# Weight sums and split weight parts made in the first half and kept in DRAM, in a two-layer kernel of split fp32 products

## The chip, the cores and the metric

The kernel runs on one core of a Trainium2 chip. The metric is the device time of one execution in microseconds (us), as the median of several runs; a profiled execution gives the trace.

## The reference

What is computed is one step of a two-layer model on 2176 tokens (128 of a prompt, 2048 latent ones) of width 1024, all in fp32. Each layer is a norm, an input projection, elementwise mixing and an output projection:

```python
for l in range(DEPTH):                       # DEPTH = 2
    shift, scale, gate = adaln(cond, w_ada[l], b_ada[l])
    h = rmsnorm(x, norm_g[l]) * (1.0 + scale) + shift
    if l % 2 == 0:                           # gated linear attention | spatial gating
        out, s_f, s_b = mix_even(h @ w_in_even[j], j, gla_init[j][0], gla_init[j][1])
    else:                                    # pooling | gated short convolution
        out = mix_odd(h @ w_in_odd[j], j)    # w_in_odd: 1024 x 3072
    out = out @ w_out[l]
    x = x + gate * out
```

## The kernel before

TensorE (PE) multiplies in a rounded fp32 format, so every fp32 operand is split: `hi` is the rounded copy (made by ACT, L207) and `lo` what is left of it (a subtraction on DVE, or every third time on POOL, L208). A product is three matmuls, hi·hi, hi·lo and lo·hi (`mm3`).

**Stage 1** (`block1`) is layer 0 up to its output projection, in four blocks of 512, 512, 512 and 640 tokens. In each block 24 weight chunks of 512 or 544 KB are loaded: 16 `w0c` chunks (one `gemm_ch` each, weights stationary) and 8 `w0t` chunks (four `gemm_tok`, two chunks each, tokens stationary). `load_w` loads a chunk into one of two `raw` slots, splits it, and the parts go into one of three `hi` and three `lo` slots. So each chunk is loaded and split four times. After each chunk `tick()` advances side work written as generators: the attention, the norm of the next block, and `adalns`, which uses the same `raw` slots. **Stage 2** (`out0`) is layer 0's output projection; it stores the new x (L998) and the norm factors `r` (L1003).

**Stage 3** is layer 1, in four blocks of tokens, processed from number 3 (named `last` in the code, though it comes first) down to 0. Its input projection is made of 12 pairs of 2 x 2 blocked products in the Strassen-Winograd form: seven products instead of eight, of sums of the operand (`operand`: tiles T from `xk` and `r`, put in `ring_t`) with sums of the weights (`Weights`: S1 to S4). In the first processed block the sums are made by four POOL operations a pair (L1096), S1 is stored unsplit (`d_s`, L1098), S2 to S4 are split and both parts stored (`d_hl`, L1113); the three later blocks load S2 to S4 as parts and S1 as sum. The quarter A11, A12, A22 parts and S1 are loaded and split in every block. The output projection then loads and splits 16 halves of `wo` (`halves`) in every block.

All these DMAs go through SP's queue (`load`). The order of instructions on each engine is set by a scheduler that plans with a timeline of its own; a queue then runs strictly in that order, so an instruction that waits holds what stands behind it. Pools of SBUF are placed one above the other (or from the right); a pool that lies over an earlier one waits, tile by tile, for that one's users.

Of the kernel before, what the change touches and what calls it, by code (L numbers as in the profile page):

```python
# [86 lines left out]
def kernel(ctx: ExitStack, tc: tile.TileContext, xT, cT, w_ada, b_ada, norm_g, final_g,  # L87
# [1544 lines left out]
```

## Time and profile before

| | us |
|---|---|
| median of 3 runs | 1966.04 (1962.41 to 1968.69) |
| profiled execution, its own time | 1955.09 |
| its span in the trace | 1953.3 |
| PE busy in the span | 1761.7 |
| DVE, ACT, POOL busy | 1323.4, 931.5, 853.0 |

The span is cut by the names of the weight tiles: stage 1 runs from 31.5 to 840 us (blocks 0 to 3: `wp` tiles with `ring` operands), stage 2 to about 1078, and stage 3 to the end; in it the pairs (`ring_t` with `wh`) and the output projections (`o_oh`, `o_ol` with `wh`) of each block take turns. A window of the trace lists for such a stretch each engine's busy time, the granted clock of PE as a share of full speed, the busy share of the 16 DMA engines and what they moved.

### The profile page before, as it was taken

Reading aid. Unit: us, or ns where it says so; the run is one execution under the profiler, and the core shown is the slowest. Engines: PE = TensorE matmul, PEld = TensorE weight load, DVE = VectorE, ACT = ScalarE, POOL = GpSimd, SP = SyncE. Lnnn points to the kernel's source line nnn. Section 1 sums busy time; section 2 is a strip of 40 time slices with the busy share of each in tenths; the row PEclk is TensorE's granted clock in tenths of the full one; section 3 lists DMA queues with packets and bytes.
Section 4 is the critical chain, followed back from the end, with each engine's and each line's share of the span. In section 5 each row is a group of like instructions: output and inputs, shape, how many; then the busy total and the mean of one; then the engine's idle time right before and its main releaser. Section 6 shows DMA issues by size and latency. Waiting matters only on the chain.

```text
span 1953.3 us, 39733 instructions
## 1 busy us (share of the span) xinstructions
PE 1761.7 (90%) x15115; PEld 1595.5 (82%) x15115; DVE 1323.4 (68%) x2335; ACT 931.5 (48%) x1900; POOL 853.0 (44%) x840
## 2 busy tenths in 40 slices
PE   5999899799989999989999487879998999899996
PEld 4886787688878888977789376769998999899996
DVE  5468737965696288667664778894768476847774
ACT  4455535564555266444443544453446354634442
POOL 0444523452343133445443677783336334542433
PEclk8999999999999999998999599989999999999998
DMA  8344434354423423556543655554975397538761
GB/s 317 109 133 147 140 103 152 111 161 136 142 86 107 145 75 109 179 187 206 166 150 102 195 193 189 199 176 129 328 229 186 116 324 246 177 103 282 237 224 50
DMA packets 190127, 329.38 MB, mean 169 GB/s; under 512 B 21488, under 2 KB 64368, under 8 KB 189936
## 3 DMA queue, kind: packets, MB, share of 16 engines
q1 hardware_dynamic: 189936, 326.84, 51.5%
q8 instruction: 119, 1.95, 0.4%
q14 instruction: 72, 0.59, 0.1%
HBM read 263.90 MB, written 62.86 MB: 167 GB/s over the span
## 4 chain that ended last, share of the span: by engine, by line
PE 54%; DVE 21%; DMA 10%; ACT 5%; issue 5%; POOL 3%; SPq 1%; DVEq 0%; ACTq 0%; POOLq 0%
PE ps_g L227 49%; DMA wp_raw<-in_w0c_dram 2%; DVE wh_lo L208 2%; DVE gl_Z L535 2%; DVE ring_t L208 2%; DVE gl_L L524 1%; DVE ring_xk L361 1%; ACT wp_hi L207 1%; DVE wp_lo L208 1%; DMA wh_raw<-in_w_dram 1%; DMA wa_wa<-in_w_ada_dram 1%; PE ps_s L327 1%; DVE oA_Sb L842 1%; DVE gl_A L587 1%; DMA ring_xk<-dr_x 1%
## 5 line engine op out<-in xcount | busy, mean ns | idle before, releaser
L227 PE MATMUL ps_g<-ring_t,wh_hi 128*128 128x272 f32 (+1 forms) x2688 | 530.2, 296 | 48.2 <-ACT ring_t L207 18.1
L227 PEld LDWEIGHTS ps_g<-ring_t,wh_hi 128*128 128x128 f32 x2688 | 430.8, 192 | 60.2 <-ACT ring_t L207 19.2
L227 PE MATMUL ps_g<-ring_t,wh_lo 128*128 128x272 f32 (+1 forms) x1344 | 388.8, 296 | 16.7 <-DVE wh_lo L208 16.0
L207 ACT ACTIVATE wh_hi<-wh_raw 128x512 fp32r<-128x512 f32 x292 | 179.2, 627 | 262.9 <-PE ps_g L227 196.7
L227 PEld LDWEIGHTS ps_g<-ring_t,wh_lo 128*128 128x128 f32 x1344 | 255.3, 192 | 22.8 <-DVE wh_lo L208 20.6
L208 DVE TENSOR_TENSOR wh_lo<-wh_raw,wh_hi 128x512 fp32r<-128x512 f32 x219 | 200.0, 922 | 84.2 <-ACT wh_hi L207 75.4
L227 PE MATMUL ps_g<-ring_hh,wp_hi 128*128 128x512 f32 (+2 forms) x632 | 234.0, 370 | 6.6 <-DVE tmp_ev L784 4.8
L227 PE MATMUL ps_g<-ring_hl,wp_hi 128*128 128x512 f32 (+2 forms) x632 | 230.6, 365 | 0.0
L227 PE MATMUL ps_g<-ring_hh,wp_lo 128*128 128x512 f32 (+2 forms) x632 | 229.5, 363 | 0.0
L281 POOL TENSOR_TENSOR tmp_acc<-tmp_acc,tmp_px 128x512 f32<-128x512 f32 (+6 forms) x83 | 108.7, 1310 | 153.5 <-ACT tmp_px L280 140.9
L227 PE MATMUL ps_g<-o_oh,wh_hi 128*128 128x272 f32 (+2 forms) x512 | 149.7, 299 | 25.7 <-ACT o_oh L207 16.4
L227 PE MATMUL ps_g<-wp_hi,ring_hh 128*128 128x256 f32 (+1 forms) x528 | 156.7, 298 | 8.6 <-ACT gl_v L711 4.4
L207 ACT ACTIVATE wp_hi<-wp_raw 128x1024 fp32r<-128x1024 f32 (+1 forms) x99 | 105.3, 1064 | 118.8 <-PE ps_g L227 41.6
L535 POOL TENSOR_TENSOR gl_Z<-gl_Z 128x128 f32<-128x128 f32 x170 | 90.4, 552 | 160.7 <-DVE gl_Z L535 107.3
L227 PE MATMUL ps_g<-o_ol,wh_hi 128*128 128x272 f32 (+2 forms) x512 | 151.9, 297 | 1.5 <-DVE o_ol L208 1.5
L227 PE MATMUL ps_g<-wp_lo,ring_hh 128*128 128x256 f32 (+1 forms) x528 | 151.9, 289 | 0.8 <-POOL wp_lo L208 0.8
L208 POOL TENSOR_TENSOR wp_lo<-wp_raw,wp_hi 128x1024 fp32r<-128x1024 f32 (+1 forms) x31 | 77.0, 2483 | 172.4 <-ACT wp_hi L207 170.9
L227 PE MATMUL ps_g<-wp_hi,ring_hl 128*128 128x256 f32 (+1 forms) x528 | 151.5, 289 | 0.7 <-DVE ring_hl L377 0.7
L227 PE MATMUL ps_g<-o_oh,wh_lo 128*128 128x272 f32 (+2 forms) x512 | 150.9, 296 | 0.0
L208 DVE TENSOR_TENSOR wp_lo<-wp_raw,wp_hi 128x1024 fp32r<-128x1024 f32 (+1 forms) x68 | 90.6, 1332 | 78.5 <-ACT wp_hi L207 78.4
L227 PEld LDWEIGHTS ps_g<-ring_hh,wp_hi 128*128 128x128 f32 x632 | 121.0, 191 | 27.8 <-DVE tmp_ev L784 5.0
L208 POOL TENSOR_TENSOR wh_lo<-wh_raw,wh_hi 128x512 fp32r<-128x512 f32 x73 | 104.4, 1431 | 88.3 <-ACT wh_hi L207 86.2
(275 smaller groups left out, 4176.3 us busy)
## 6 DMA issues: line engine op xcount, KB each, us to landing
wh_raw<-in_w_dram SPq DMA_DIRECT2D x156, 256.0 KB, 3.5
wp_raw<-in_w0c_dram SPq DMA_DIRECT2D x64, 512.0 KB, 4.0
wh_hi<-dr_hl SPq DMA_DIRECT2D x108, 256.0 KB, 3.4
wh_lo<-dr_hl SPq DMA_DIRECT2D x108, 256.0 KB, 3.9
wp_raw<-in_w_ada_dram SPq DMA_DIRECT2D x32, 512.0 KB, 3.8
wh_raw<-in_wo_dram SPq DMA_DIRECT2D x64, 256.0 KB, 3.3
dr_hl<-wh_hi SPq DMA_DIRECT2D x36, 256.0 KB, 2.2
dr_hl<-wh_lo SPq DMA_DIRECT2D x36, 256.0 KB, 2.0
```

Of the source, the lines that this page charges most:

```text
L207: act(out=hi, in_=src, func=AF.Copy)
L208: (eng or lo_engine()).tensor_tensor(out=lo, in0=src, in1=hi.bitcast(F32), op=ALU.subtract)
L227: mm(out=out, lhsT=a, rhs=b, start=start and i == 0, stop=stop and i == n - 1, skip_group_check=resumed)
L281: eng.tensor_tensor(out=acc, in0=acc, in1=sq, op=ALU.add)
L327: mm(out=acc[32 * g:32 * g + 32, 0:w], lhsT=sc[:, k, :], rhs=wt[:, g * w:(g + 1) * w], start=k == 0, stop=k == KT - 1, tile_position=(0, 3 ...
L361: dve.scalar_tensor_tensor(out=xt[:, a:b], in0=xt[:, a:b], scalar=gs[:, l, k, cd:cd + 1], in1=r[:, a:b], op0=ALU.mult, op1=ALU.mult)
L524: dve.tensor_tensor(out=L, in0=qk, in1=L, op=ALU.mult)
L535: (dve if i >= 2 or s < 4 else gps).tensor_tensor(out=dst, in0=dst, in1=bc(src), op=ALU.add)
L587: dve.copy_predicated(out=A[rr_, :, rr_], mask=notl[rr_].unsqueeze(1).to_broadcast([32, 4, 32]), data=D[rr_])
L842: dve.scalar_tensor_tensor(out=S[64:P, h, 0:P], in0=Sb[0][64:P, h, 0:P], scalar=S[64:P, h, P:P + 1], in1=S[64:P, h, 0:P], op0=ALU.mult, op ...
```

## The change

1. `load_w` gets a key. For w0c chunks 4 to 15 the parts made in block 0 are stored to DRAM, for the 8 w0t chunks and w0c 0 to 3 those made in block 1: 24 chunks, 48 stores of 512 or 544 KB. Later uses (12 in block 1, 24 each in blocks 2 and 3) load the two parts straight into `hi` and `lo`: 60 loads and 60 splits become 120 loads.
2. A generator `weight_sums` makes S1 to S4 of all 12 pairs, three ticks a pair, started in block 1 after its mixer: two 512 KB loads into both `raw` slots, four sums on POOL, three copies on ACT, three subtractions on DVE, and seven stores of 256 KB. It has 36 ticks: the last 8 of block 1, the 24 of block 2, the first few of block 3.
3. Stage 3's first block then does as the later ones. `raw` has 5 slots instead of 7, `hi` and `lo` 7 instead of 6.
4. The first block of stage 3 stores the 32 split parts of its `wo` halves (`d_wo`, 256 KB each), and the three later ones load parts: 48 splits less, 48 loads more.
5. Pools change places: `xs2` lies below `tmp2`; `ring2` directly above `wh` and below `tmp3`, which then lies where stage 2's `xs2` and `tmp2` were; `yp` and `yo` come from the right.

```diff
+    d_w = {}
+    def load_w(src, n, key=None, keep=False):
+        hi = wp.tile([P, WMAX], F32R, tag="hi", bufs=NHI)[:, 0:n]
+        lo = wp.tile([P, WMAX], F32R, tag="lo", bufs=NLO)[:, 0:n]
+        if key in d_w:
+            for z, d in zip((hi, lo), d_w[key]):
+                load(out=z.bitcast(F32), in_=d)
+            return hi, lo
         raw = raw_tile()[:, 0:n]
         load(out=raw, in_=src[:, 0:n])
-        hi = wp.tile([P, WMAX], F32R, tag="hi", bufs=NHI)
-        lo = wp.tile([P, WMAX], F32R, tag="lo", bufs=NLO)
-        split(raw, hi[:, 0:n], lo[:, 0:n])
-        return hi[:, 0:n], lo[:, 0:n]
+        split(raw, hi, lo)
+        if keep:
+            d_w[key] = [dr.tile([P, n], F32, tag=f"w{len(d_w)}{z}") for z in "hl"]
+            for z, d in zip((hi, lo), d_w[key]):
+                load(out=d, in_=z.bitcast(F32))
+        return hi, lo
...
+    def weight_sums():
+        for i in range(len(PAIRS)):
+            x, y = raw_tile(), raw_tile()
+            for z, row in ((x, 0), (y, 1)):
+                load(out=z[:, 0:1024], in_=w1[PAIRS[i][row]])
+            A11, A12, A21, A22 = (z[:, a:a + 512] for z in (x, y) for a in (0, 512))
+            yield 1
+            gps.tensor_tensor(out=A22, in0=A21, in1=A22, op=ALU.add)
+            gps.tensor_tensor(out=A21, in0=A11, in1=A21, op=ALU.subtract)
+            gps.tensor_tensor(out=A11, in0=A22, in1=A11, op=ALU.subtract)
+            gps.tensor_tensor(out=A12, in0=A12, in1=A11, op=ALU.subtract)
+            load(out=d_s[i], in_=A22)
+            yield 1
+            for j, s_ in enumerate((A11, A21, A12)):
+                hi = tmp.tile([P, 640], F32R, tag="px", bufs=2)[:, 0:512]
+                act(out=hi, in_=s_, func=AF.Copy)
+                lo = s_.bitcast(F32R)
+                dve.tensor_tensor(out=lo, in0=s_, in1=hi.bitcast(F32), op=ALU.subtract)
+                for z, d in zip((hi, lo), d_hl[i][j]):
+                    load(out=d, in_=z.bitcast(F32))
+            yield 1
...
         finish(mixer)
+        if bi == 1:
+            side(sums_, 1)
...
     finish(ada_)
+    finish(sums_)
...
+    xs = pool("xs2", stack=s2, reuse_waits="tile")
     tmp = pool("tmp2", stack=s2, reuse_waits="tile")
-    xs = pool("xs2", stack=s2, reuse_waits="tile")
...
+    ring = pool("ring2", stack=s3, reuse_waits="tile")
     tmp = pool("tmp3", stack=s3, reuse_waits="tile")
...
+    def weight(i, name):
+        if name in ("S2", "S3", "S4"):
+            hl = hl_half()
+            for z, d in zip(hl, d_hl[i][int(name[1]) - 2]):
+                load(out=z.bitcast(F32), in_=d)
             return hl
+        return split_half(raw_half(d_s[i] if name == "S1" else half_src(i, name)))
...
         def halves(c):
-            return [split_half(raw_half(wo[1, c][:, 512 * i:512 * i + 512])) for i in range(2)]
+            out = []
+            for i in range(2):
+                if bi + 1 == NB2:
+                    out.append(split_half(raw_half(wo[1, c][:, 512 * i:512 * i + 512])))
+                    for z, d in zip(out[-1], d_wo[c][i]):
+                        load(out=d, in_=z.bitcast(F32))
+                else:
+                    out.append(hl_half())
+                    for z, d in zip(out[-1], d_wo[c][i]):
+                        load(out=z.bitcast(F32), in_=d)
+            return out
```

## Rows read from the trace of the kernel before

**Rows 1.** The first page of the profile: the span, PE's busy time, and over the span in 40 equal slices PE's busy tenths and what the DMA engines moved.

```profile
span 1953.3 us, 39733 instructions
...
PE 1761.7 (90%) x15115; PEld 1595.5 (82%) x15115; DVE 1323.4 (68%) x2335; ACT 931.5 (48%) x1900; POOL 853.0 (44%) x840
...
PE   5999899799989999989999487879998999899996
...
GB/s 317 109 133 147 140 103 152 111 161 136 142 86 107 145 75 109 179 187 206 166 150 102 195 193 189 199 176 129 328 229 186 116 324 246 177 103 282 237 224 50
```

**Rows 2.** Windows of stage 3: the pairs of block 3 (the first two rows), its output projection, the pairs and the output projection of block 2, and the output projection of block 1. In brackets is the number of instructions.

```profile
core 0: us, PE busy (x) PEld busy (x) DVE busy (x) ACT busy (x) POOL busy (x), PEclk, DMA share, GB/s
1094.80:1117.00 22.20, 14.64 (x44) 10.61 (x44) 20.78 (x27) 13.73 (x33) 18.42 (x18) 0.50 0.41 120
1117.00:1296.70 179.70, 142.81 (x958) 132.08 (x959) 152.17 (x176) 80.50 (x164) 138.27 (x110) 0.93 0.53 184
1296.70:1357.30 60.60, 53.45 (x410) 52.70 (x409) 35.39 (x59) 26.77 (x52) 29.74 (x24) 0.94 0.44 136
1357.20:1486.80 129.60, 127.46 (x990) 125.62 (x988) 88.18 (x145) 65.00 (x130) 53.53 (x53) 1.00 0.80 268
1486.80:1555.80 69.00, 57.79 (x427) 57.45 (x427) 45.69 (x72) 29.49 (x58) 32.09 (x30) 0.90 0.37 118
...
1685.90:1753.30 67.40, 58.26 (x425) 57.70 (x426) 44.35 (x77) 30.55 (x63) 32.35 (x32) 0.92 0.33 107
```

**Rows 3.** Groups of instructions in the pairs of block 3 (1117 to 1296.7 us): tile written and read, count, busy time and mean of one, and the idle time of that engine ahead of them with what ended it.

```profile
L227 PE MATMUL ps_g<-ring_t,wh_lo 128*128 128x272 f32 x314 | 94.6, 308 | 16.1 <-DVE wh_lo L208 15.6 <-POOL wh_lo L208 0.5
L208 DVE TENSOR_TENSOR wh_lo<-wh_raw,wh_hi 128x512 fp32r<-128x512 f32 x58 | 67.5, 1187 | 10.5 <-ACT wh_hi L207 10.1
L1096 POOL TENSOR_TENSOR wh_raw<-wh_raw,wh_raw 128x512 f32<-128x512 f32 x43 | 67.0, 1566 | 6.2 <-issue 1.4 <-DMA dr_hl<-wh_hi 1.3 <-DVE tmp_ev L1245 1.3
...
L207 ACT ACTIVATE wh_hi<-wh_raw 128x512 fp32r<-128x512 f32 x79 | 45.9, 621 | 37.3 <-POOL wh_raw L1096 22.8 <-DMA wh_raw<-in_w_dram 10.8 <-DVE tmp_ev L1262 3.8
L208 POOL TENSOR_TENSOR wh_lo<-wh_raw,wh_hi 128x512 fp32r<-128x512 f32 x19 | 29.0, 1527 | 15.4 <-ACT wh_hi L207 15.3
```

**Rows 4.** The same view for the pairs of block 2 (1357.2 to 1486.8 us).

```profile
L208 DVE TENSOR_TENSOR wh_lo<-wh_raw,wh_hi 128x512 fp32r<-128x512 f32 x34 | 29.3, 862 | 13.3 <-ACT wh_hi L207 12.6
```

**Rows 5.** The instructions on the tile `wh_lo`, minimum, median and maximum of one in ns: in the pairs of block 3, and then in those of block 2.

```profile
L208 DVE TENSOR_TENSOR wh_lo<-wh_raw,wh_hi x58: 672/1258/1828, 1120.0 to 1292.9; 128x512 fp32r<-128x512 f32 x58
...
L208 DVE TENSOR_TENSOR wh_lo<-wh_raw,wh_hi x34: 675/693/1599, 1359.4 to 1486.2; 128x512 fp32r<-128x512 f32 x34
```

**Rows 6.** From stage 2 to stage 3: PE's timeline at its first pair product (in brackets the idle time before it and what ended it); SP's timeline of DMA issues (start, us, engine, line, tiles, count); and the window between the two stages, with the columns of Rows 2.

```profile
1094.81 0.59 PE L227 MATMUL ps_g<-ring_t,wh_hi 128*128 128x272 f32 x1 [16.77 <-ACT ring_t L207]
...
1072.85 0.42 SPq L1133 DMA_DIRECT2D tmp_r<-dr_r  x1
...
1077.21 3.81 SPq L1489 DMA_DIRECT2D yp_ys<-dr_x  x8
1082.07 0.32 SPq L1003 DMA_DIRECT2D dr_r<-tmp_r  x1
...
1087.68 1.38 SPq L1140 DMA_DIRECT2D ring_xk<-dr_x  x3
...
1078.00:1094.80 16.80, 0.04 (x1) 0.00 (x0) 7.96 (x11) 6.00 (x11) 7.68 (x7) 0.54 0.99 334
```

**Rows 7.** PE's waits in the output projection of block 2 (total us, times, longest).

```profile
PE ps_g L227 <- ACT o_oh L207: 6.0, 1, 6.0
PE ps_g L227 <- DVE tmp_ev L1214: 5.2, 1, 5.2
```

**Rows 8.** Windows of stage 1, with the columns of Rows 2: its blocks 0, 2 and 3.

```profile
31.50:224.70 193.20, 181.92 (x1932) 150.75 (x1928) 134.62 (x261) 97.98 (x197) 78.90 (x78) 0.97 0.45 142
...
414.40:599.90 185.50, 177.27 (x1839) 147.94 (x1837) 130.13 (x259) 101.75 (x211) 75.34 (x80) 0.98 0.42 130
599.90:840.00 240.10, 224.77 (x2557) 205.93 (x2556) 157.67 (x345) 118.20 (x266) 81.89 (x103) 0.99 0.39 119
```

**Rows 9.** The page's groups of the splits of stage 1's chunks, and two rows of its list of DMA issues (count, size, median us from issue to landing).

```profile
L207 ACT ACTIVATE wp_hi<-wp_raw 128x1024 fp32r<-128x1024 f32 (+1 forms) x99 | 105.3, 1064 | 118.8 <-PE ps_g L227 41.6
...
L208 POOL TENSOR_TENSOR wp_lo<-wp_raw,wp_hi 128x1024 fp32r<-128x1024 f32 (+1 forms) x31 | 77.0, 2483 | 172.4 <-ACT wp_hi L207 170.9
...
L208 DVE TENSOR_TENSOR wp_lo<-wp_raw,wp_hi 128x1024 fp32r<-128x1024 f32 (+1 forms) x68 | 90.6, 1332 | 78.5 <-ACT wp_hi L207 78.4
...
wp_raw<-in_w0c_dram SPq DMA_DIRECT2D x64, 512.0 KB, 4.0
wh_hi<-dr_hl SPq DMA_DIRECT2D x108, 256.0 KB, 3.4
```

**Rows 10.** Two windows with the busiest DMA engines within the pairs of blocks 2 and 1, with the columns of Rows 2.

```profile
1367.00:1416.00 49.00, 47.03 (x366) 46.21 (x365) 36.99 (x64) 24.55 (x49) 18.01 (x18) 1.00 0.95 329
1563.00:1611.00 48.00, 46.03 (x355) 44.99 (x354) 37.07 (x66) 25.04 (x52) 15.76 (x17) 1.00 0.93 326
```

**Rows 11.** SP's waits at L1113, the stores of split sums, from 1078 to 1296.7 us (total us, times, longest).

```profile
SPq L1113 <- ACT wh_hi L207: 41.8, 21, 4.1
SPq L1113 <- DVE wh_lo L208: 28.1, 18, 3.7
...
SPq L1113 <- POOL wh_lo L208: 9.2, 8, 1.6
```

More of the change, by code (lines that the diff above doesn't have):

```diff
@@ L648, in gla_tile, with gemm_tok @@
         yield 1
-    def gemm_tok(src, ncol, h, nt):
-        halves = [load_w(src[i], 4 * ncol) for i in range(2)]
+    def gemm_tok(j, ncol, h, nt, keep):
+        halves = [load_w(w0t[j][i], 4 * ncol, ("t", j, i), keep) for i in range(2)]
         for i in range(nt):
@@ L691, in first_units, with half_src @@
         return len(wq)
+    d_s = [dr.tile([P, 512], F32, tag=f"s{i}") for i in range(12)]
+    d_hl = [dr.tile([3, 2, P, 512], F32, tag=f"hl{i}") for i in range(12)]
+    ORDER = [(hh, z) for hh in range(4) for z in ("pool u conv" if hh == 3 else "u pool conv").split()]
+    ROWS = {"u": (2, 3), "pool": (0, 1), "conv": (4, 5)}
+    PAIRS = [tuple(6 * hh + r for r in ROWS[z]) for hh, z in ORDER]
+    def half_src(i, name):
+        j = 512 * (int(name[2]) - 1)
+        return w1[PAIRS[i][int(name[1]) - 1]][:, j:j + 512]
+    def weight_sums():
[19 more added lines that the diff above has]
+            yield 1
     def block1(bi):
@@ L725, in block1 @@
             c0 = 0
-            for i, o in gemm_tok(w0t[0], 272, h, nt):
+            for i, o in gemm_tok(0, 272, h, nt, bi == 1):
                 tok0(i, o)
         for c in range(c0, 4):
-            for a, b, o in gemm_ch(w0c[c], h, 0, n):
+            for a, b, o in gemm_ch(w0c[c], h, 0, n, c, bi == 1):
                 qk0(c, a, b, o)
-        for i, o in gemm_tok(w0t[1], 272, h, nt):
+        for i, o in gemm_tok(1, 272, h, nt, bi == 1):
             act(out=v[i][:, 240:512], in_=o, func=AF.Copy)
@@ L741, in block1 @@
         for u in range(2):
-            for i, o in gemm_tok(w0t[2 + u], 256, h, nt):
+            for i, o in gemm_tok(2 + u, 256, h, nt, bi == 1):
                 dve.tensor_copy(out=vs[:, i, 2 * u:2 * u + 2, :],
@@ L773, in block1 @@
         for hh in range(4):
-            for a, b, o in gemm_ch(w0c[12 + hh], h, 0, n):
+            for a, b, o in gemm_ch(w0c[12 + hh], h, 0, n, 12 + hh, bi == 0):
                 x = silu_psum(o, b - a, gps, pre=glag[:, 0:1])
@@ L1027 @@
     o1 = pool("o1", stack=late, reuse_waits="tile", right=True)
-    yp = pool("yp", stack=late, reuse_waits="tile", right=True)
     s4 = ExitStack()
-    ring = pool("ring2", stack=s4, reuse_waits="tile")
+    yp = pool("yp", stack=s4, reuse_waits="tile", right=True)
     width[:] = [TMAX, 552, 7, 3, 2, 3]
@@ L1038, in raw_half @@
     def raw_half(src=None):
-        raw = wh.tile([P, 512], F32, tag="raw", bufs=7)
+        raw = wh.tile([P, 512], F32, tag="raw", bufs=5)
         if src is not None:
@@ L1046, in hl_half @@
     def hl_half():
-        return tuple(wh.tile([P, 512], F32R, tag=z, bufs=6) for z in ("hi", "lo"))
+        return tuple(wh.tile([P, 512], F32R, tag=z, bufs=7) for z in ("hi", "lo"))
     def split_half(raw):
@@ L1409, in in1 @@
             if p:
-                if last:
-                    p.w.load("A11", "A12", "A21")
                 p.m1()
@@ L1423, in in1 @@
             if p:
-                if last:
-                    p.w.load("A22")
-                    p.w.sums()
                 p.m5()
@@ L1430, in in1 @@
             old_p = p
+    d_wo = [dr.tile([2, 2, P, 512], F32, tag=f"wo{c}") for c in range(KT)]
     def block(bi):
@@ L1460, in block @@
             s4.close()
-            yo = pool("yo", stack=s4, reuse_waits="tile")
+            yo = pool("yo", stack=s4, reuse_waits="tile", right=True)
             Y = yo.tile([P, KT, n], F32, tag="y")
```

54 lines of the change are left out of this document (7 added, 47 removed).

## Prediction

> **What bounds the kernel now.** I read the first page, then the windows by stage, then within the one odd stretch the groups of instructions and the waits. PE is busy for 1761.7 of 1953.3 us [rows 1], so the shares say "PE-bound" and hide where the rest goes. The windows of stage 3 show it. The pairs of block 2 take 129.6 us for 990 matmuls, with PE busy 127.46 at a granted clock of 1.00. The same pairs in block 3, which comes first, take 22.2 + 179.7 = 201.9 us for 1002 [rows 2]. The products are the same; what block 3 does besides is to make the sums. In its window POOL is busy 138.27 of 179.7 us, DVE 152.17 and PE 142.81. The groups say why: POOL spends 67.0 us on L1096, ACT's copies stand idle 22.8 us behind it, and PE's hi·lo products wait 15.6 us for `wh_lo` [rows 3]. One subtraction on DVE costs 1187 ns there against 862 in block 2 [rows 3, 4], with equal minima (672 and 675) and medians of 1258 and 693 [rows 5]. So this stretch is bound by the making of weights on POOL, DVE and ACT, with PE waiting. Three other places have gaps: the change from stage 2 to 3, with PE idle for 16.77 us while the DMA engines run at a share of .99 [rows 6]; the head of each output projection (6.0 + 5.2 us in block 2) [rows 7]; and stage 1, where blocks 2 and 3 lose 185.5 - 177.27 = 8.2 and 240.1 - 224.77 = 15.3 us [rows 8]. Stage 1 is where the new work is put; it is bound by PE, so little can be won there and much lost.
>
> **The pairs of block 3** (the sums and 36 splits leave, parts are loaded as in the later blocks). The first 44 matmuls, up to 1117 us, wait for the operand at half clock and do so still. The other 958 took 179.7 us, 188 ns each; in block 2 one takes 129.6 / 990 = 131 ns, so 958 take 125.4 us: **-54**. The new load is that of block 2, 10 x 256 KB a pair at 268 GB/s [rows 2]; five `raw` slots for four splits a pair are enough, and `hi` and `lo` gain one. Ends: -58 (PE-bound with no loss, 127.46 / 990) and -45 (block 3 starts with empty slots).
>
> **From stage 2 to stage 3.** The first `xk` load of the operand was issued at 1087.68, behind eight loads of `ys` and a store that waited [rows 6]. Both leave its way in part: `ring2` now lies over `wr` and `oB`, free earlier, and no sum store is ahead. Against that `r` and T lie in `tmp3` over stage 2's own `tmp2` and `xs2`, so `r` waits for its last users, where it was loaded at 1072.85. What then comes last is the making of the operand on DVE. Of 16.77 us I take **-5** (0 to -12).
>
> **Output projections of layer 1.** Blocks 2, 1 and 0 lose 16 copies and 16 subtractions each (16 x .63 on ACT, some 11 x .86 on DVE), and gain 16 loads that the DMA engines have room for (a share of .37). PE's gaps there hang on DVE's elementwise work and ACT's `o_oh` [rows 7], which come earlier with less ahead of them: some 2 to 3 us a block, **-6** (0 to -14). Block 3 adds 32 stores behind splits on SP's queue, at some 2 us of landing, and its window has 60.6 - 53.45 = 7.2 us of gaps [rows 2]: **+2** (0 to +6).
>
> **Stage 1, what it gains.** In blocks 2 and 3 all 24 splits go, in block 1 half: for a block 24 x 1.06 = 25 us of ACT, 16 x 1.33 = 21 of DVE, 8 x 2.48 = 20 of POOL [rows 9]. Nearly all of it lay beside PE's work. Of the 23.5 us of gaps in blocks 2 and 3 [rows 8] I give back **-6** (0 to -20).
>
> **Stage 1, what it pays.** (a) *Bytes.* A direct chunk is 1.05 MB in place of .52. In block 2 that adds 24 x .53 = 12.7 MB, and eight pairs of sums add 8 x (1.05 + 7 x .26) = 23 MB. Over 185.5 us these are 192 GB/s beside the 130 there now: 322 GB/s. The most that any window shows is 334 at a share of .99 [rows 6], or 329 at .95 [rows 10]. By the bytes that a unit of share carries in such windows of large pieces (some 340), the share goes from .42 to about .98 for the 36 ticks of the sums (62 + 185 + 40 us). In the two windows of rows 10, at .95 and .93, PE still lost only 49 - 47.03 = 2.0 and 48 - 46.03 = 2.0 us, 4% where the whole stretch lost 1.7%. At 4% of 287 us less some that is lost anyway: **+10** (0 to +30).
> The Trainium skill (page HBM Reference, section Specifications (TRN2)) says that a core streaming alone measures about 425 GB/s. By that figure the load would be .76 of what can be had and term (a) near 0; no window here comes above 334, at a share of .99, so the sum goes by the row.
> (b) *Slots.* A direct load has no stage but the three `hi` and `lo` slots. Between two `gemm_tok` the next second half needs a slot that the present gemm frees with its last tile. Before, the copy and the subtraction had to follow then, 1.06 + 1.33 us [rows 9]; now two loads of 512 KB, 4.0 us or more. Two such places a block, in blocks 2 and 3, at some 2 us: **+8** (0 to +16).
> (c) *SP's queue.* 84 stores of sums, and the 48 of chunks, wait on SP for a split; behind them stand the next chunk's loads. In block 3 of layer 1 such stores held SP for 41.8 + 28.1 + 9.2 = 79 us in 47 waits, 1.7 us each [rows 11]. With two chunks in store most is hidden: **+4** (0 to +25).
> (d) *POOL and DVE.* In block 2 the sums put 8 x 4 x 1.57 = 50 us on POOL, and 20 of splits leave: 75 + 30 = 105 of 185.5 us. DVE gains 24 subtractions and loses 16 larger ones, and stays near 130 [rows 8]. Rows 3 to 5 say that a busy POOL makes DVE's two-operand work up to 1.8 times as long; even all 30 us on DVE make 160 of 185.5. PE's share of that: **+2** (0 to +10).
> The Trainium skill (page SBUF — State Buffer, section SBUF: two separate sides) says that a DVE operation with two SBUF inputs and a GpSimd one that reads SBUF exclude each other for a whole instruction. The equal minima and the medians of rows 5 agree. By it the 74 us of sums (48 x 1.55) are not made free by a move, but go where DVE has room. The sum is as in (d).
>
> **Sum.** -54 - 5 - 6 + 2 - 6 + 10 + 8 + 4 + 2 = -45. The profiled execution took 1955.09 us, so 1910 by its measure; the median of the runs shown is 10.95 above it, so 1921.
>
> **Rivals.**
> *Slower: stage 1 becomes bound by DMA.* In a tick of the sums' stretch (185.5 / 24 = 7.73 us) the queue has to move 1.05 MB of chunk, .96 of sums and .47 of the rest, 2.48 MB. At 322 GB/s it just fits. If the mix of loads, stores and attention's short pieces is served at only 250, a tick takes 9.9 us: 36 x 2.2 = 79 us, with (b) to (d) 93, and the time is 1966 - 69 + 93 = 1990. It decides from a loss of 69 us in stage 1 on, at a rate of some 260. For it: nothing over 200 us long shows more than 268. Against: that one was set by PE (127.46 of 129.6), and rows 10 show 326 to 329 kept for 48 us. Also some of the sums can slide to ticks where less is asked.
> *Stage 1 gives back much, not all:* the high ends of (a) to (c) in part, 25 to 50 us more than the sum: 1945 to 1964.
> *The pairs of block 3 don't get faster,* being held by the operand, cold slots or the new place of T: only -15 to -20 of the 54, so 1957 or so. Against: the waits of rows 3 are for weights.
> *More gain:* DMA hides all, and relief on DVE and ACT closes more gaps: -65 to -80, 1886 to 1900.
>
> **Chances.** The forecast (1900 to 1945) .61, stage 1 giving back much .14, slower .11, pairs not faster .04, more gain .10. The range takes in the forecast, more gain in most and half of the next: 1893 to 1957. A measurement of this kernel tells about 0.3% from no change, that is 1960 to 1972: faster .82, same .06, slower .12.
>
> **What would show it.** Right: the pairs of block 3 at about 150 us with POOL near 55 of them; `r` no later than 1080 on the old scale; block 2 of stage 1 at 185 to 200 us with a DMA share of .9 or more and no single wait of PE above 4 us. Wrong: PE waits for loads of `wp_hi` or `wp_lo` in most chunks of blocks 2 and 3, SP's waits at the stores of sums of several us with chunk loads behind them, or a first pair product later than now after stage 2's end.

## The result

The changed kernel takes 1946.18 us (1942.66 to 1947.14, four runs) against 1964.22 (1960.24 to 1968.69) for the kernel before, measured beside it: a ratio of 0.9904, with an interval of 0.9878 to 0.9931. It is faster, but by 18 us and not by 45. Its profiled execution took 1945.44 us, near its median. That of the kernel before, 1955.09, lay 9 us under its own, so the two traces differ by only 9.7 us of span; the steps below are counted in the traces.

The first page of the profile after, as in [rows 1]:

```profile
span 1943.6 us, 39900 instructions
...
PE 1760.2 (91%) x15115; PEld 1602.0 (82%) x15115; DVE 1201.7 (62%) x2268; ACT 851.5 (44%) x1792; POOL 748.3 (38%) x799
...
PE   5999999988968899998889949998999999999996
...
GB/s 318 109 177 261 287 265 261 278 281 290 277 225 226 249 244 147 149 201 197 210 155 154 98 188 245 247 251 229 305 249 232 196 318 246 234 163 324 238 209 101
```

PE's busy time is the same, the DMA engines move 225 to 290 GB/s in slices 4 to 15 where they moved 75 to 161, and in slice 12, inside stage 1, PE falls to 6 tenths. Windows after: blocks 0, 2 and 3 of stage 1, the wait before stage 3, then pairs and output projection of stage 3's blocks 3 and 2 (columns of [rows 2]):

```profile
31.50:233.00 201.50, 188.62 (x1923) 153.82 (x1925) 133.65 (x260) 100.08 (x199) 75.24 (x78) 0.95 0.62 209
421.90:638.60 216.70, 184.79 (x1838) 152.69 (x1836) 136.35 (x268) 89.74 (x206) 94.65 (x100) 0.91 0.76 264
638.60:893.60 255.00, 234.95 (x2604) 218.80 (x2603) 144.26 (x339) 104.21 (x259) 76.64 (x107) 0.95 0.59 191
1122.90:1146.70 23.80, 1.04 (x2) 0.58 (x2) 7.98 (x13) 6.60 (x14) 3.02 (x4) 0.55 0.83 300
1146.70:1290.70 144.00, 136.52 (x984) 131.81 (x984) 100.53 (x162) 73.48 (x153) 65.15 (x71) 0.92 0.71 225
1290.70:1358.80 68.10, 56.64 (x425) 56.26 (x425) 45.05 (x74) 29.27 (x58) 32.63 (x28) 0.92 0.71 235
1358.80:1489.10 130.30, 127.51 (x990) 126.16 (x988) 88.77 (x145) 64.35 (x130) 51.48 (x52) 1.00 0.81 274
1489.10:1549.50 60.40, 55.59 (x426) 54.97 (x426) 32.78 (x59) 20.99 (x43) 28.11 (x26) 0.97 0.58 188
```

Beside [rows 2] and [rows 8]: the pairs of block 3 went from 201.9 to 144.0 us, and PE is busy 136.52 of them. Block 2 of stage 1 went from 185.5 to 216.7 us, with no more matmuls (1838) at a mean granted clock of .91 for .98. Block 3 of stage 1 can't be set beside [rows 8], which cut it at 840 us: its last chunk product before ends at 848.7.

The table takes the end of the last chunk product of each stage-1 block, the first pair product and the span from the traces; the kernels behind the first two are the experiments.

| us | block 0 | 1 | 2 | 3 | first pair | span |
|---|---|---|---|---|---|---|
| before | 222.9 | 412.5 | 597.1 | 848.7 | 1094.8 | 1953.3 |
| after | 231.5 | 420.1 | 636.8 | 893.6 | 1146.7 | 1943.6 |
| e1 sums only | 224.0 | 436.6 | 717.9 | 992.5 | 1244.0 | 2041.5 |
| e2 chunks only | 230.2 | 410.9 | 588.0 | 834.7 | 1082.6 | 1943.3 |
| e3 four ticks | 228.2 | 416.5 | 613.5 | 864.2 | 1115.1 | 1909.7 |
| e4 wo split | 230.9 | 419.2 | 636.2 | 896.4 | 1147.4 | 1960.2 |
| e5 bytes only | 230.2 | 414.8 | 592.0 | 834.5 | 1086.3 | 1884.0 |
| e6 no stores | 229.7 | 418.6 | 617.7 | 858.7 | 1107.8 | 1904.7 |
| e7 five ticks | 230.3 | 418.2 | 611.6 | 862.3 | 1111.1 | 1911.7 |
| e8 kept in 1 | 222.4 | 416.4 | 614.8 | 875.7 | 1123.1 | 1920.1 |
| e9 sums on DVE | 229.9 | 406.8 | 600.0 | 844.6 | 1098.6 | 1897.1 |
| e10 sums, no splits | 229.9 | 418.4 | 617.4 | 869.3 | 1122.2 | 1920.7 |
| e11 splits, no sums | 227.3 | 412.5 | 594.9 | 846.0 | 1100.9 | 1898.5 |
| e12 pool order | 230.8 | 414.3 | 611.5 | 859.2 | 1107.9 | 1906.8 |
| e13 fills | 230.4 | 421.7 | 611.3 | 855.4 | 1107.4 | 1902.0 |
| e14 ys on ACT | 231.6 | 409.3 | 602.2 | 849.1 | 1102.5 | 1899.5 |

Kernels e4, e5, e6, e10, e11 and e13 were executed once each. Kernels e9, e12 and e14 have the same stage 1, with its instructions in the same order, and end it at 844.6, 859.2 and 849.1 (the traced execution of e12, 1908.73 us, was the longest of its five): differences under some 15 us between two single traces say little there. One thing no run holds fixed: the scheduler orders each kernel anew, so that from the first sums on the other instructions of POOL, ACT and DVE stand in another order in e3, e5, e6, e9, e10, e11 and e13 than in the kernels that they are compared with. What part of a difference that makes is not known.

From before to after: stage 1 +44.9, stage 2 +3.4 (229.3 for 225.9), the gap from the last product of stage 2 up to the first pair product +3.6 (23.8 for 20.2), the pairs of block 3 -57.9, their output projection +7.6 (68.1 for 60.5), and all the rest of stage 3 -11.3.

**Where block 2 loses.** One stall in full, from the timelines of SP, POOL, ACT, DVE and PE of the changed kernel (in brackets the idle time before and what ended it):

```profile
521.00 0.33 SPq L728 DMA_DIRECT2D wp_raw<-in_w_dram  x1
...
526.14 0.33 SPq L728 DMA_DIRECT2D wp_raw<-in_w_dram  x1
...
533.77 1.28 POOL L732 TENSOR_TENSOR wp_raw<-wp_raw 128x512 f32<-128x512 f32 x1 [9.57 <-DMA wp_raw<-in_w_dram]
...
538.10 1.15 ACT L740 ACTIVATE tmp_px<-wp_raw 128x512 fp32r<-128x512 f32 x2 [8.41 <-POOL wp_raw L734]
...
540.78 0.62 ACT L515 ACTIVATE gl_Z<-gl_Z 128x512 f32<-128x512 f32 x1
...
544.25 0.63 ACT L740 ACTIVATE tmp_px<-wp_raw 128x512 fp32r<-128x512 f32 x1 [2.85 <-DMA dr_hl<-tmp_px]
544.79 0.42 ACT L530 ACTIVATE gl_Q<-gl_Z 128x256 f32<-128x256 f32 x1
...
545.72 0.42 DVE L533 TENSOR_TENSOR gl_Q<-gl_qk,gl_Q 128x256 f32<-128x256 f32 x1
...
546.29 0.47 PE L558 MATMUL ps_m<-gl_Q,gl_qk 64*32 64x64 f32 x16 [10.31 <-DVE gl_Q L533]
```

The load of the second half of a pair's weights is issued at 526.14. POOL's next instruction in order is the first sum; it stands for 9.57 us until the load has landed. ACT's next is the copy of a sum, which stands 8.41 us for POOL, and behind it are the attention's ACT steps (L515). The third copy of the pair stands another 2.85 us, until a store has freed one of the two `px` slots, ahead of the attention's next ACT step (L530), whose result its DVE step (L533) reads; PE has stood for 10.31 us when the attention's product follows.

This is one stall of several. PE's three largest waits in block 2 (421.9 to 638.6 us; total us, times, longest), and two windows with the columns of [rows 2]:

```profile
PE ps_m L558 <- DVE gl_Q L533: 10.3, 1, 10.3
PE ps_s L270 <- ACT tmp_nw L207: 7.4, 1, 7.4
PE ps_m L564 <- DVE gl_L L535: 3.1, 2, 1.8
...
538.00:558.50 20.50, 8.86 (x80) 6.73 (x81) 16.39 (x34) 12.58 (x26) 11.43 (x14) 0.50 0.66 217
...
596.00:606.20 10.20, 6.14 (x72) 4.78 (x73) 7.73 (x15) 7.08 (x17) 4.08 (x7) 0.50 0.96 338
```

The second wait isn't the attention's but that of the norm of the next block, whose copy on ACT stands behind copies of sums and steps of the attention. Within each of these two stalls PE's granted clock falls to .50, the lower of its two levels (1.2 GHz): for 20.5 us from 538.0 and for 10.2 us from 596.0. So of the 31 us that block 2 grew by some 24 are PE standing, and 7.5 are the same matmuls at the lower clock.

Over 355 to 640 us the waits of POOL, and of SP at the loads and stores of sums (total us, times, longest), are:

```profile
POOL wp_raw L732 <- DMA wp_raw<-in_w_dram: 46.5, 4, 27.7
...
SPq L728 <- DMA dr_hl<-wp_raw: 22.5, 8, 5.1
SPq L744 <- ACT tmp_px L740: 19.5, 9, 5.1
...
SPq L744 <- ACT gl_Q L530: 3.9, 2, 3.5
```

### The profile page after: what moved, and what is told of

It reads as the page before. It is cut to its first block, busy times and chain, and to the rows that moved or that the text cites. A ratio compares the mean times of both kernels' runs of the same rounds, so it can differ in the third digit from the quotient of the medians.

```text
span 1943.6 us, 39900 instructions
## 1 busy us (share of the span) xinstructions
PE 1760.2 (91%) x15115; PEld 1602.0 (82%) x15115; DVE 1201.7 (62%) x2268; ACT 851.5 (44%) x1792; POOL 748.3 (38%) x799
## 4 chain that ended last, share of the span: by engine, by line
PE 44%; DVE 11%; DMA 7%; issue 2%; ACT 2%; SPq 1%; POOL 1%; DVEq 0%; ACTq 0%; POOLq 0%
PE ps_g L238 42%; DMA oA_Sb<-dr_ub 1%; DVE ring_t L208 1%; DVE ring_xk L372 1%; DVE oA_Sb L898 1%; PE ps_s L1328 1%; DVE gl_Z L546 1%; DMA wh_lo<-dr_hl 1%; DMA ring_xk<-dr_x 1%; DMA dr_hl<-wp_raw 1%; DMA wh_hi<-dr_hl 1%; DMA wh_raw<-in_w_dram 1%; DVE yp_ys L1536 1%; DVE tmp_T L1165 0%; DVE wh_lo L208 0%
## 5 line engine op out<-in xcount | busy, mean ns | idle before, releaser
L238 PEld LDWEIGHTS ps_g<-ring_t,wh_hi 128*128 128x128 f32 x2688 | 428.7, 190 | 39.9 <-ACT ring_t L207 23.9
L238 PE MATMUL ps_g<-ring_hh,wp_hi 128*128 128x512 f32 (+2 forms) x632 | 239.8, 379 | 11.5 <-DVE tmp_ev L840 8.0
L238 PE MATMUL ps_g<-ring_hh,wp_lo 128*128 128x512 f32 (+2 forms) x632 | 234.9, 372 | 4.6 <-DVE wp_lo L208 3.9
L238 PE MATMUL ps_g<-ring_hl,wp_hi 128*128 128x512 f32 (+2 forms) x632 | 234.9, 372 | 0.0
L207 ACT ACTIVATE wh_hi<-wh_raw 128x512 fp32r<-128x512 f32 x208 | 130.8, 629 | 214.7 <-PE ps_g L238 185.1
L238 PE MATMUL ps_g<-o_oh,wh_hi 128*128 128x272 f32 (+2 forms) x512 | 148.0, 295 | 22.5 <-ACT o_oh L207 11.4
L208 DVE TENSOR_TENSOR wh_lo<-wh_raw,wh_hi 128x512 fp32r<-128x512 f32 x156 | 118.3, 761 | 56.2 <-ACT wh_hi L207 45.6
L238 PEld LDWEIGHTS ps_g<-ring_hh,wp_lo 128*128 128x128 f32 x632 | 123.8, 196 | 23.1 <-DVE wp_lo L208 4.5
L238 PEld LDWEIGHTS ps_g<-ring_hl,wp_hi 128*128 128x128 f32 x632 | 124.1, 196 | 16.4 <-issue 1.8
L546 POOL TENSOR_TENSOR gl_Z<-gl_Z 128x128 f32<-128x128 f32 x170 | 85.0, 518 | 136.3 <-DVE gl_Z L546 87.5
L530 ACT ACTIVATE gl_L<-gl_Z 128x256 f32<-128x256 f32 x204 | 82.9, 419 | 103.7 <-DVE gl_Z L546 74.5
L238 PEld LDWEIGHTS ps_g<-o_oh,wh_hi 128*128 128x128 f32 x512 | 97.8, 194 | 23.9 <-ACT o_oh L207 12.0
```

The lines of the kernel that those rows point to most:

```text
L207: act(out=hi, in_=src, func=AF.Copy)
L208: (eng or lo_engine()).tensor_tensor(out=lo, in0=src, in1=hi.bitcast(F32), op=ALU.subtract)
L238: mm(out=out, lhsT=a, rhs=b, start=start and i == 0, stop=stop and i == n - 1, skip_group_check=resumed)
L530: act(out=dst.rearrange("p (b t s) -> p t b s", t=2, s=s), in_=diag_ap(Z, 2 * i, s), func=AF.Exp, scale=1.0 / 16.0)
L546: (dve if i >= 2 or s < 4 else gps).tensor_tensor(out=dst, in0=dst, in1=bc(src), op=ALU.add)
```

## The experiments

My theory H: the sums' operations wait in their engines' in-order queues, and the attention's steps (and, as the waits above show, the norm's) stand behind them. The rivals: B, the bytes fill the DMA engines; S, three slots are too few for direct loads.

**e1, the sums without the kept chunks.**

```diff
     def load_w(src, n, key=None, keep=False):
+        keep = False
```

> The changed kernel, but no chunk of stage 1 is kept: every chunk is loaded and split in every block as before; the sums, stage 3, wo and the pools are as changed. Theory H (the sums' operations on POOL, ACT and DVE wait in their in-order queues for the sums' own loads and stores, and the attention's steps stand behind them): block 2 of stage 1 still takes 25 to 32 us more than the 185.5 of before, block 0 returns to 193, and the time is some 1935 to 1946. Rival B (bytes: chunks as parts fill the DMA engines): block 2 comes back to within 10 us of before at a DMA share near .7, and the time is 1910 to 1922. Rival S (three slots for direct loads hold PE): as B, with PE's waits at wp_hi and wp_lo gone.

Measured: 2039.84 us, 1.0394 of before (1.0377 to 1.0411). No theory had it, H (1935 to 1946) included. PE's and SP's waits from 420 to 860 us:

```profile
PE ps_g L239 <- ACT wp_hi L207: 73.6, 12, 18.9
...
SPq L745 <- ACT tmp_px L741: 38.8, 21, 5.2
...
SPq L225 <- DMA dr_hl<-wp_raw: 26.2, 13, 4.4
```

PE waits 73.6 us for copies of chunks: chunks and sums now share the two `raw` slots, and a chunk's load (L225) stands behind a pair's stores. So the kept chunks look like more than a saving: from block 2 on they free the `raw` slots. Without them moving the sums loses 78 us against the kernel before (1962.1 beside it). This says nothing on B.

**e2, the kept chunks alone** (the kernel before with part 1 of the change, its `load_w` and the keys of its callers).

> The kernel before with part 1 alone: chunks of stage 1 kept and loaded as parts; sums still made in stage 3. H: block 0 pays for its 24 stores (some 8 us), blocks 1 to 3 stay within 6 us of before together or gain from fewer splits; the time is 1962 to 1974. B or S: blocks 2 and 3 together lose 20 to 35 us and the time is 1985 to 2000.

Measured: 1941.66 us, 0.9892 (0.9867 to 0.9916). Block 0 pays 7.3 us; blocks 1 to 3 *gain* 21.3 (189.6 to 180.7, 184.6 to 177.1, 251.6 to 246.7). That is better than H's 1962 to 1974. Doubling the bytes of a chunk with three slots costs nothing that can be seen, so S falls. Part 1 alone is as fast as the whole change. By difference from the changed kernel, the sums cost stage 1 893.6 - 834.7 = 58.9 us, 39.6 of them in block 2, and give back 57.9 in the pairs.

The window from 355 to 640 us, and there the attention's DVE product on 128 x 512, first after, then e2:

```profile
355.00:640.00 285.00, 241.90 (x2519) 199.47 (x2518) 192.73 (x377) 124.59 (x270) 123.72 (x132) 0.91 0.76 265
...
L535 DVE TENSOR_TENSOR gl_L<-gl_qk,gl_L 128x512 f32<-128x512 f32 x34 | 34.1, 1014 | 6.1 <-ACT gl_L L530 3.3 <-ACT gl_qk L773 2.6
```

```profile
355.00:640.00 285.00, 276.25 (x2868) 234.85 (x2867) 151.00 (x357) 115.23 (x267) 72.04 (x104) 0.99 0.59 199
...
L535 DVE TENSOR_TENSOR gl_L<-gl_qk,gl_L 128x512 f32<-128x512 f32 x32 | 24.8, 788 | 6.3 <-ACT gl_L L530 4.1 <-ACT gl_qk L730 2.1
```

**e3, four ticks a pair.**

```diff
             yield 1
+            yield 1
             gps.tensor_tensor(out=A22, in0=A21, in1=A22, op=ALU.add)
```

> The changed kernel with one more tick between the loads of a pair's halves and its sums on POOL (four ticks a pair, 48 in all, so the sums run on into block 3). H: the loads have landed when POOL comes to the sums, POOL and ACT wait less ahead of the attention, and the loss of block 2 (31 us) falls by half: 1925 to 1936. B and S: the bytes are spread over a third more time, a gain of 5 us at most: 1940 to 1946.

Measured: 1917.81 us, 0.9781 (0.9740 to 0.9821). One line takes off 28 us, more than H's 1925 to 1936; stage 1 ends 29.4 sooner, half of the sums' cost. ACT's waits for POOL's sums from 330 to 720 us fall from 23.4 to 12.0.

**e4, wo split in every block.**

```diff
         def halves(c):
-            out = []
...
+            return [split_half(raw_half(wo[1, c][:, 512 * i:512 * i + 512])) for i in range(2)]
```

> The changed kernel with wo's halves loaded and split in every block of stage 3, as before, and none stored. If the shorter output projections come from the splits that left, block 3's falls from 68 to about 61 us and those of blocks 2, 1 and 0 rise from 60, 62 and 52 to about 69, 67 and 54: the sum 6 us longer than the changed kernel. If they come from something else (the pools' new order, the places of yp and ring2), they stay near 60 and 62 and the time falls by some 7.

Measured: 1962.0 us in a single execution, 16 us over the changed kernel where 6 were expected. From the end of a block's pairs to the next, or to the end, it takes 69.2, 66.5, 66.9 and 70.7 us, where the changed kernel takes 68.1, 60.4, 62.3 and 69.3: in the last three, 12 us are the splits'. Block 3's doesn't shorten without the 32 stores, so these cost nothing that can be seen. PE's waits in block 3's output projection, after and then in e4:

```profile
PE ps_g L238 <- ACT o_oh L207: 7.7, 1, 7.7
PE ps_g L238 <- DVE tmp_ev L1243: 3.7, 1, 3.7
```

```profile
PE ps_g L238 <- ACT o_oh L207: 5.2, 1, 5.2
PE ps_g L238 <- DVE tmp_ev L1243: 3.8, 1, 3.8
```

Before, the slow pairs left DVE and ACT the time to finish block 3's elementwise work beside them. Now it stands at the end, as in block 2 before [rows 7]. That is read from the waits, not tried.

**e5, the bytes without the work.**

```diff
-            gps.tensor_tensor(out=A22, in0=A21, in1=A22, op=ALU.add)
...
             load(out=d_s[i], in_=A22)
             yield 1
             for j, s_ in enumerate((A11, A21, A12)):
...
-                act(out=hi, in_=s_, func=AF.Copy)
...
-                dve.tensor_tensor(out=lo, in0=s_, in1=hi.bitcast(F32), op=ALU.subtract)
-                for z, d in zip((hi, lo), d_hl[i][j]):
-                    load(out=d, in_=z.bitcast(F32))
+                for d in d_hl[i][j]:
+                    load(out=d, in_=s_)
```

> The changed kernel with the sums' loads and stores kept, byte for byte and in the same ticks, but without the four sums, three copies and three subtractions of a pair (the stores take the loaded quarters as they are, so layer 1's sums are left out of the computation). H: what costs is the operations' waits in the queues of POOL, ACT and DVE; without them stage 1 ends at 835 to 855 and the time is 1890 to 1908. B: bytes cost; stage 1 ends at 885 to 895 as in the changed kernel (893.6), time 1938 to 1946.

Measured: 1885.82 us, just under H's range, stage 1 ending at 834.5, where e2 has 834.7. Its window from 355 to 640 us:

```profile
355.00:640.00 285.00, 273.79 (x2833) 231.80 (x2832) 150.73 (x358) 114.97 (x265) 71.33 (x104) 0.98 0.90 314
```

The DMA engines ran 285 us at 314 GB/s and a share of .90, and PE is busy 273.79 us of them, for 276.25 in e2. B falls: all of the 59 us hang on the ten operations of a pair.

**e6, the sums without their stores.**

```diff
-            load(out=d_s[i], in_=A22)
+            if i == 0:
+                load(out=d_s[i], in_=A22)
...
-                for z, d in zip((hi, lo), d_hl[i][j]):
+                for z, d in zip((hi, lo), d_hl[i][j] if i == 0 else ()):
```

> The changed kernel with the sums' loads and operations kept, but their seven stores only for the first pair (stage 3 reads the first pair's for all, so the other pairs' weights are left out). H: POOL and ACT still wait for loads; only waits for stores go (slots of px and raw); stage 1 ends at 870 to 890. B: 1.8 of 2.9 MB a pair are gone, stage 1 ends at 850 to 862.

Measured: 1906.44 us, stage 1 ending at 858.7, within B's numbers and not H's. With e5 beside it, it isn't the bytes alone, since these cost nothing without the operations. I read it as the stores holding slots, as the `px` store does in the stall above, so that ACT and POOL wait. That is argued, not shown. From 355 to 640 us POOL's waits for the sums' loads fall only from 46.5 to 31.2 us, and ACT's for POOL's sums from 21.5 to 9.1, while SP, which stood 22.5 us at L728 for stores, now stands there 43.7 us for the subtraction that frees a `raw` slot.

**e7, five ticks** (e3, and:)

```diff
             load(out=d_s[i], in_=A22)
             yield 1
+            yield 1
```

> The changed kernel with five ticks a pair: one more between loads and sums, one more between sums and splits (60 ticks, of which 56 are there, so the last pair is made after block 3's ticks). H: as the four ticks a pair, and ACT no longer waits for POOL's sums (12 us there): another 5 to 12 us off, 1906 to 1914; against it the last pair's work may stand alone at the end of stage 1 (up to 8 us). B: the same as with four, 1914 to 1922.

Measured: 1917.63 us, 0.9778 (0.9737 to 0.9820), the same as four. That is B's number and not H's. ACT's waits for POOL's sums (330 to 720 us) fall again, from 12.0 to 6.9 us, and buy nothing, so they are not what is left of the cost.

**e8, four ticks, all 24 chunks stored in block 1, sums started with block 2.**

```diff
-            for a, b, o in gemm_ch(w0c[12 + hh], h, 0, n, 12 + hh, bi == 0):
+            for a, b, o in gemm_ch(w0c[12 + hh], h, 0, n, 12 + hh, bi == 1):
...
-        if bi == 1:
-            side(sums_, 1)
...
+        if bi == 2:
+            side(sums_, 1)
```

> Four ticks a pair, the sums started with block 2 (48 ticks, blocks 2 and 3), and all 24 chunks stored in block 1, none in block 0. If the 24 stores of block 0 cost its 7 to 9 us, block 0 ends at 223 again (231 in the changed kernel); block 1 splits 12 chunks more and stores 24 more, but has no sums beside it: 0 to +8. Block 2 and 3 hold all of the sums: the cost that the four-tick kernel has (30 us to the end of stage 1) stays within 5. Time 1908 to 1922.

Measured: 1921.59 us, 0.9795 (0.9771 to 0.9818). Block 0 ends at 222.4 again, as before the change, so its 24 stores and their waits cost 7 to 8 us; block 1 then takes 194.0 us (188.3 in e3) and block 3 260.9 (250.7). Nothing is won.

**e9, the sums on DVE** (e3, and in all four sums:)

```diff
-            gps.tensor_tensor(out=A22, in0=A21, in1=A22, op=ALU.add)
+            dve.tensor_tensor(out=A22, in0=A21, in1=A22, op=ALU.add)
```

> Four ticks a pair, with the four sums of a pair on DVE in place of POOL (DVE is busy 188 of 285 us there, POOL 118). If what is left of the cost (30 us to the end of stage 1) is POOL's: its two-operand sums holding DVE's operations, and the attention's POOL steps behind them, stage 1 ends at 840 to 852 and the time is 1893 to 1906. If it is the waits for loads and stores in whichever queue, or DVE's own load, it stays at 860 to 870 or gets worse: 1915 to 1930.

Measured: 1903.02 us, 0.9691 (0.9652 to 0.9730): 15 us off e3, stage 1 ending at 844.6. From 355 to 640 us:

```profile
355.00:640.00 285.00, 267.03 (x2768) 223.65 (x2768) 196.26 (x449) 135.02 (x304) 87.64 (x118) 0.98 0.80 279
...
L535 DVE TENSOR_TENSOR gl_L<-gl_qk,gl_L 128x512 f32<-128x512 f32 x34 | 24.6, 735 | 1.7 <-ACT gl_L L530 1.7
...
PE ps_s L270 <- ACT tmp_nw L207: 9.0, 1, 9.0
```

DVE does more (196.26 us busy for 192.73 after) and PE loses less (busy 267.03 us for 241.90; one tick and the engine together). On POOL the sums cost more, although it was the emptier engine. The last line is PE's longest wait there: it is the norm's, 9.3 us in e3 too and none in e2. So the largest single stall that is left in block 2 has moved from the attention to the norm, and neither the tick nor the engine takes it away.

**e10 and e11, sums without splits and splits without sums.** e10 is e3 with

```diff
...
-                act(out=hi, in_=s_, func=AF.Copy)
...
-                dve.tensor_tensor(out=lo, in0=s_, in1=hi.bitcast(F32), op=ALU.subtract)
-                for z, d in zip((hi, lo), d_hl[i][j]):
-                    load(out=d, in_=z.bitcast(F32))
+                for d in d_hl[i][j]:
+                    load(out=d, in_=s_)
```

and e11 is e3 less the four `gps.tensor_tensor`.

> Four ticks a pair, the four sums on POOL kept, the three copies and subtractions of a pair left out (the stores write the unsplit sums twice, so the split of layer 1's sums is left out of the computation). If POOL's sums carry the cost, stage 1 still ends at 855 to 866; if the splits on ACT and DVE carry it, at 835 to 845.

> Four ticks a pair, the four sums left out and the copies and subtractions kept (quarters are split and stored as loaded, so layer 1's sums are left out of the computation). The mirror of the run before: 835 to 845 at the end of stage 1 if POOL's sums carry the cost, 855 to 866 if the splits do. If each alone costs little, the chain of both, sum then split then store within the ticks, is the cost.

Measured: 1922.5 us with the sums on POOL alone, stage 1 ending at 869.3; 1900.26 with the splits alone, ending at 846.0. Where e3 still pays 29.5 us over e2, the sums alone pay 34.6 and the splits alone 11.3, which is within the spread: POOL's sums carry most of it.

**e12, e9 with the pools of stages 2 and 3 in their old order** (part 5 undone, `yo` from the left too).

```diff
-    xs = pool("xs2", stack=s2, reuse_waits="tile")
     tmp = pool("tmp2", stack=s2, reuse_waits="tile")
+    xs = pool("xs2", stack=s2, reuse_waits="tile")
...
-    ring = pool("ring2", stack=s3, reuse_waits="tile")
     tmp = pool("tmp3", stack=s3, reuse_waits="tile")
...
+    yp = pool("yp", stack=late, reuse_waits="tile", right=True)
     s4 = ExitStack()
-    yp = pool("yp", stack=s4, reuse_waits="tile", right=True)
+    ring = pool("ring2", stack=s4, reuse_waits="tile")
```

> The kernel of the sums on DVE with the pools of stages 2 and 3 in the order of the kernel before (part 5 undone). If the first pair product comes late because r now lies over stage 2's last tiles, and its load stands on SP behind the loads of ys (issued 1090.3, 15 us after the last store of stage 2), r is loaded by 1077 on that scale again, the xk loads wait a little longer for their place, and the gap of 20.5 us ahead of the first product falls to 10 to 15: 5 to 10 us off, 1893 to 1899. If the gap is the making of the operand, whatever the order, it stays at 19 to 22 and the time at 1900 to 1906. The other way, xk over stage 2's last tiles stands behind more loads than r did: 1904 to 1910.

Measured: 1898.73 us, 0.9673 (0.9657 to 0.9689), not told apart from e9. The time lies in the first range, but the gap doesn't shrink: PE's idle time ahead of the first pair product is 19.3 us, and 20.5 in e9. The place of the tiles decides which load is last, not when. SP's timeline after, with DVE's and PE's first steps of stage 3:

```profile
1125.93 1.32 SPq L1150 DMA_DIRECT2D ring_xk<-dr_x  x3
...
1134.55 3.24 SPq L1506 DMA_DIRECT2D yp_ys<-dr_x  x6
1138.13 0.32 SPq L1143 DMA_DIRECT2D tmp_r<-dr_r  x1
...
1144.07 2.18 DVE L372 SCALAR_TENSOR_TENSOR ring_xk<-ring_xk,cst_gs,tmp_r 128x544 f32<-128x544 f32 x3 [12.71 <-DMA tmp_r<-dr_r]
...
1146.71 0.59 PE L238 MATMUL ps_g<-ring_t,wh_hi 128*128 128x272 f32 x1 [20.24 <-ACT ring_t L207]
```

and in e12:

```profile
1083.27 0.42 SPq L1144 DMA_DIRECT2D tmp_r<-dr_r  x1
...
1095.91 3.39 SPq L1507 DMA_DIRECT2D yp_ys<-dr_x  x6
1099.65 1.67 SPq L1151 DMA_DIRECT2D ring_xk<-dr_x  x3
```

After, `xk` is loaded early and `r` last, behind the `ys` loads; DVE stands 12.71 us for it. In e12 `r` is early (1083.27) and `xk` last (1099.65), behind the same `ys`. The gap from the last stage-2 product to the first pair product is 22.9 us there and 23.9 in e9.

**e13, fills for sums** (e3, and:)

```diff
-            gps.tensor_tensor(out=A22, in0=A21, in1=A22, op=ALU.add)
...
+            for z, times in ((A22, 3), (A21, 2), (A11, 3), (A12, 2)):
+                for _ in range(times):
+                    gps.memset(z, 0.5)
```

> Four ticks a pair, with POOL's four sums replaced by ten fills of the same quarters with a constant (some 0.53 us each, so about as long in all, after the same loads and with the same successors, but reading no SBUF; layer 1's sums are left out of the computation). If POOL's sums cost by holding DVE's two-operand operations, the fills don't: DVE's time above the minimum of each form is some 18 us in 355 to 640 us (36 with the sums, 18 without), and stage 1 ends at 842 to 850. If they cost by standing in POOL's queue ahead of the attention's steps, waiting for loads, the fills do too: stage 1 ends at 858 to 868.

Measured: 1903.78 us, stage 1 ending at 855.4, between the two. I add up, over DVE's instructions that start from 355 to 640 us, the time of each above the shortest of its line and shape: before 33.6 us, e2 14.7, after 41.1, e3 36.4, e9 17.9, e10 30.8, e11 17.9, and with the fills 14.5. So POOL's sums do stretch DVE's work, by some 20 us, and fills, which read no SBUF, don't. What the stretch costs in time is not shown: stage 1 ends 8.8 us sooner with fills than with sums, and 9.4 later than with neither (e11), both within the spread of single traces. Block 2 ends at 611.3 with fills, 613.5 with sums and 594.9 with neither, which points to the place in the queue; but e12, with no sums on POOL, ends it at 611.5 too. How the rest divides between stretch, place and the scheduler's order stays open.

**e14, the `ys` loads of the first block on ACT's queue** (e9, and:)

```diff
-            load(out=y, in_=d_x1[c][:, t0:t1])
+            (nc.scalar.dma_start if bi + 1 == NB2 else load)(out=y, in_=d_x1[c][:, t0:t1])
```

> The kernel of the sums on DVE, with the eight loads of ys of stage 3's first block issued on ACT's queue in place of SP's. If the load of r comes late because it stands behind them on SP, r is loaded 4 to 8 us sooner and the gap ahead of the first pair product (20.5 us) shrinks to 12 to 17; time 1894 to 1900. If r waits for its place in SBUF, or for the DMA engines, the gap stays: 1900 to 1906. ACT could also stand at such an issue: up to 5 us more.

Measured: 1901.32 us, 0.9691 (0.9669 to 0.9713), the gap 22.7 us. SP's timeline:

```profile
1084.06 2.75 SPq L1151 DMA_DIRECT2D ring_xk<-dr_x  x3
...
1093.18 1.33 SPq L1100 DMA_DIRECT2D wh_raw<-in_w_dram  x3
1094.56 0.42 SPq L1144 DMA_DIRECT2D tmp_r<-dr_r  x1
```

`r` still goes out at 1094.56, now behind weight loads. That the `ys` loads on SP set it falls. What does is not settled. A rival that I didn't test: from the last product of stage 2 to the first pair product some 6.5 MB move before the change (1074.6 to 1094.8 us) and 7.1 after (1122.9 to 1146.7), at 320 and 300 GB/s with the DMA engines at a share of .95 and .83, so that whichever load is last may wait for the bytes ahead of it.

## Why the prediction was wrong

The direction was right; the time, 1946, lies in the range (1893 to 1957), in the rival "stage 1 gives back much, not all" (1945 to 1964). The forecast's gain was 2.5 times the real one. That the time still fell in the range is luck: in stage 1 slots, bytes and fewer splits together cost 26 us less than their terms (-14.0 in e2 for -6 + 8 + 10 = +12), and the sums' operations 53 us more. Nor was it for that rival's reason, the high ends of (a) to (c) in part (whose 25 to 50 us more make 1946 to 1971, not 1945 to 1964). Two of the signs of being wrong did show: SP's waits at the stores of sums (up to 5.1 us), and a first pair product later after stage 2's end (20.24 us of idle time for 16.77).

*Pairs of block 3, -54:* right, -57.9. PE is busy 136.52 of 144.0 us.

*Stage 1, what it gains, -6, and (b) slots, +8:* the wrong sign together. e2 shows 21 us gained in blocks 1 to 3 with the same three slots. I had counted what splits leave ACT, DVE and POOL as busy time, and most of it as hidden; but DVE's time above the shortest of each shape (under e13) falls from 33.6 to 14.7 us, so they were also in the way. How much of the 21 us that is, no run shows. The 24 stores of block 0, put under (c), cost 7 us.

*(a) bytes, +10, and the rival "bound by DMA":* nothing. e5 moves the same bytes at a share of .90 and ends stage 1 where e2 does. By the figure of the Trainium skill (page HBM Reference, section Specifications (TRN2)), about 425 GB/s for a core streaming alone, the term was near 0, and e5 agrees with that; the figure itself is reached in no window shown here.

*(c) SP's queue, +4, and (d) POOL and DVE, +2:* this is the step that failed. The ten operations of a pair cost 58.9 us, ten times as much. I set the sums' 50 us against POOL's free time (105 of 185.5 us) and found room. The room was there: POOL is busy 94.65 of block 2's 216.7 us. But POOL, ACT and DVE run their instructions in order, as the stall above shows, and the chains of the attention and of the norm pass through the same queues on their way to PE: what I left out of the price is how long the sums' operations wait there, for loads, for each other and for slots, and what stands behind them. Giving the loads one tick more (e3) takes half of the cost away. Of the 30 us left, moving the sums from POOL to DVE (e9) takes 15 by the medians; the rest is not divided. The granted clock adds to it: at a mean of .91 block 2's matmuls are busy 184.79 us for 177.27, 7.5 us more for the same matmuls.
The Trainium skill (page SBUF — State Buffer, section SBUF: two separate sides) says that a DVE operation with two SBUF inputs and a GpSimd one that reads SBUF exclude each other for a whole instruction, and e13 agrees: fills of about the same length leave DVE's work unstretched (14.5 us above the shortest, for 36.4 with sums). I had said that this would go where DVE has room. Whether it did is not shown: e6 has as much of it as the changed kernel (43.4 us for 41.1) and ends stage 1 35 us sooner.

*From stage 2 to stage 3, -5:* +3.6, the wrong sign. I named that `r` would wait for stage 2's last users and still took a gain. `r` went out at 1138.13, 14.5 us after the last store of x of stage 2; before, at 1072.85 [rows 6], it was 2.5 us ahead of that store. e12 and e14 move the order of loads and not the gap; its cause stays open.

*Output projections, -6 and +2:* -11.3 for all that follows block 3's, within the range given; e4 lays 12 us there to the splits. Block 3's own is +7.6, above its range, and not by its stores (e4).

## What to carry to other kernels

Work moved beside other work is priced by what its instructions wait for and who stands behind them in each in-order queue, not by busy shares: put its loads a step further ahead of its use, and try it on another engine, be it the busier one. Test the idea in halves: the sums moved without the kept chunks lost 78 us to the kernel before, the kept chunks alone had the whole gain of the change, and with one more tick and the sums on DVE both together took off 3.1% (1903.02 us), with the old pool order 3.3% (1898.73). A resource near its limit in a window is not yet a price: in e5 a DMA share of .90 over 285 us cost nothing.

## What was not expected of the hardware

The DMA engines kept 314 GB/s for 285 us, loads and stores mixed, at a share of .90, with PE at 273.79 of 285 us busy (276.25 in e2). And with the splits of chunks gone from POOL (2.48 us each) and DVE, DVE's time above the shortest fell from 33.6 to 14.7 us (355 to 640 us). Only 2.4 of the 33.6 us lay in DVE's own splits; most of it lay in the attention's instructions (12.0 and 5.5 us in its two largest groups).
